# Attention by pairs of heads: scores in row halves of the array, feature-major values, bias tables by VectorE

## The chip, the cores and the metric

One core of one Trainium2 chip runs the whole program. The metric is device time in microseconds (us). All arithmetic is fp32, or fp32 split into a high and a low part (fp32r, "hi" and "lo", three matmuls for one product).

## The reference

Two layers of a trunk over 512 latent tokens (an 8 x 64 grid) of width 1024, with 256 context tokens. Layer 0 runs a state-space part (S5) beside neighbourhood attention with 8 heads of 64; layer 1 is a Fourier mixing. Each layer ends in a squared-ReLU MLP. The change concerns the attention alone:

```
scale = DH ** -0.5
s_lat = jnp.einsum('brqhd,brkhd->bhrqk', qg, k_blk).astype(f32) * scale + bias[None]
s_lat = jnp.where(mask, s_lat, NEG_INF)
s_ctx = jnp.einsum('brqhd,bkhd->bhrqk', qg, k_c).astype(f32) * scale
p = jax.nn.softmax(jnp.concatenate([s_lat, s_ctx], axis=-1), axis=-1).astype(v_l.dtype)
o = (jnp.einsum('bhrqk,brkhd->brqhd', p[..., :n_lat], v_blk)
     + jnp.einsum('bhrqk,bkhd->brqhd', p[..., n_lat:], v_c))
```

`bias` is a learned table by relative position, `mask` the window of 16 columns.

## The kernel before

**Stages.** After the norms, the projection by `w_in` (`qkv_gen`) runs on PE, interleaved with the S5 blocks (`s5_gen`), which are heavy on DVE. Then comes the attention (`na_gen`), interleaved with the gated unit of the S5 output (`glu_gen`) and with the loads and the row sum of one modulation vector (`side_gen`, `gemv_row`, tile `gacc`). Then the output projection (`wout_mm`, tile `po` with `whi`, `mh`), then the MLP. The order of the instructions on each engine is set by a scheduler from the order in which the generators emit them; every engine then works strictly in that order, waiting on semaphores.

**Attention.** The 512 queries are 4 column tiles (`ct`) of 128; each has 192 (`ct` 0 and 3) or 256 local keys and 256 context keys. One step of `scores` is one head: the tile `qP` holds each head's 64 features with zeros in the other 64 rows, so that q of one head times the 128 rows of two heads' keys gives one head's scores (L711 context, L712 local). DVE takes a minimum (L714), adds the bias table and takes the minimum again (L716); ACT takes the exponential (L717). `turn` transposes the 4 blocks of 128 keys on PE (L723, tile `ptp`) and ACT copies them (L724). `values` multiplies with the transposed scores as the stationary operand (L731, tile `po`). After 8 heads DVE divides by the sums (L735), and `to_mix` transposes to feature-major on PE (L741) and splits into hi and lo. PSUM has 3 banks for scores and outputs while S5 runs (`psum(mm=2, py=1, q=3)`), then 5.

**Bias tables.** Three tables are made once (L679 to L684): ACT copies the relative-position table with its sign turned, and POOL issues a DMA that adds the mask, broadcast over 8 heads, onto it from DRAM. The tables and the work tiles lie in the two large tiles `fh` and `fl`, which hold the projection's input (`lh`, `ll`) until its last matmul. The third large tile, `acc` (`RM`), holds the raw table; later the GLU's operand `gHL` takes its place.

**Weight slots.** `W.raw` has two slots of 1 MB in this stage. Four blocks of `w_mod` (each read by two DVE multiply-adds, L209) go through them, then the quarters of `w_out`, which ACT casts (L66) and DVE subtracts (L70).

Of the kernel before, what the change touches and what calls it, by code (L numbers as in the profile page):

```python
# [19 lines left out]
S = 512  # L20
# [73 lines left out]
def trunk(tc, I, out, dump=None):  # L94
# [15 lines left out]
    with es:  # L110
# [336 lines left out]
        qP = gp.tile([128, 4, 2, S], F32, name="qP")  # L447
# [24 lines left out]
        def qkv_gen():  # L472
            for grp in (4, 5, 6, 7, 2, 3):
                if grp == 2:
                    for b in range(2):
                        P.memset(qP[b * 64:b * 64 + 64, :, 1 - b], 0.0)
# [4 lines left out]
                if kind in "qk":  # L481
                    for m in range(2):
# [4 lines left out]
                        if kind == "q":  # L487
                            for b in range(2):
# [29 lines left out]
        def s5_params(b):  # L518
# [17 lines left out]
            qf = qP.rearrange("p m b n -> p (m b n)")  # L536
# [4 lines left out]
            if b == 2:  # L541
                CA = qf[:, 1024:2176].rearrange("p (c g e h) -> p c g e h", c=2, g=4, e=9)
            else:
                CA = s5b.tile([128, 2, 4, 9, 16], F32, tag="CA", name="CA", bufs=2)

# [127 lines left out]
        def na_gen():  # L673
            RM = big("acc", F32, "RM")
            SY.dma_start(RM[:, 0:2048], I["rb"])
            Rv = RM[:, 0:2048].rearrange("p (h a f) -> p h a f", a=4, h=8)
            N0, N1 = big("fh", F32, "N0"), big("fl", F32, "N1")
            bias = []
            for v, a0, na, bt in ((0, 1, 3, N0[:, 2048:3584]), (1, 0, 4, N0[:, 0:2048]), (2, 0, 3, N1[:, 0:1536])):  # L679
                bt = bt.rearrange("p (h n) -> p h n", h=8)  # L680
                A.activation(bt, Rv[:, :, a0:a0 + na].rearrange("p h a f -> p h (a f)"), AF.Copy, scale=-1.0)
                P.dma_start(bt, I["mask"][:, v, None, a0 * 64:(a0 + na) * 64].to_broadcast([128, 8, na * 64]),
                            accum_op=ADD)
                bias.append(bt)  # L684
            ots = [N0[:, 2048 + i * 512:2560 + i * 512] for i in range(4)]
            pes = [N1[:, 1536 + i * 512:2048 + i * 512] for i in range(3)]
            pTs = [N1[:, 3072 + i * 512:3584 + i * 512].rearrange("p (j n) -> p j n", j=4) for i in range(2)]
# [14 lines left out]
            def scores(i):  # L702
                ct, h = divmod(i, 8)
                bt, nl, k0, _ = cts[ct]
                w = nl + C
                if h == 0:
                    sums[ct] = sml.tile([128, 8], F32, tag="sm", name="sm")
                mt = h // 2
                sc = ps_q("sc")
                qs = qP[:, mt, h % 2, ct * 128:ct * 128 + 128]  # L710
                T.matmul(sc[:, nl:w], qs, kcT[:, mt], start=True, stop=True)  # L711
                T.matmul(sc[:, 0:nl], qs, kT[:, mt, k0:k0 + nl], start=True, stop=True)  # L712
                nc_ = sml.tile([128, 1], F32, tag="nc", name="nc")
                V.tensor_reduce(nc_, sc[:, nl:w], AX.X, MIN)  # L714
                nm = sml.tile([128, 1], F32, tag="nm", name="nm")
                V.tensor_tensor_reduce(sc[:, 0:nl], sc[:, 0:nl], bt[:, h], 1.0, nc_, ADD, MIN, nm)  # L716
                A.activation(pes[i % 3][:, 0:w], sc[:, 0:w], AF.Exp, bias=nm, scale=-1.0,  # L717
                             accum_out=sums[ct][:, h:h + 1])

            def turn(i):  # L720
                pt = ps_t("ptp").rearrange("p (j n) -> p j n", j=4)
                for j, (o, _, _) in enumerate(cts[i // 8][3]):
                    T.transpose(pt[:, j], pes[i % 3][:, o:o + 128], ident)  # L723
                A.copy(pTs[i % 2], pt)  # L724

            def values(i):
                ct, h = divmod(i, 8)
                if h == 0:
                    outs[ct] = ps_q("po").rearrange("p (h d) -> p h d", h=8)
                for j, (_, kn, vv) in enumerate(cts[ct][3]):  # L730
                    T.matmul(outs[ct][:, h], pTs[i % 2][0:kn, j], vv[:, h * 64:h * 64 + 64], start=(j == 0), stop=(j == 3))  # L731
                if h == 7:
                    rs = sml.tile([128, 8], F32, tag="rs", name="rs")
                    V.reciprocal(rs, sums[ct])
                    V.tensor_tensor(ots[ct].rearrange("p (h d) -> p h d", h=8), outs[ct],  # L735
                                    rs[:, :, None].to_broadcast([128, 8, 64]), MULT)

            def to_mix(ct):
                pt = ps_t("pto").rearrange("p (j n) -> p j n", j=4)
                for j in range(4):  # L740
                    T.transpose(pt[:, j], ots[ct][:, j * 128:j * 128 + 128], ident)  # L741
                split_to(mix["h"][:, 4:8, ct * 128:ct * 128 + 128], mix["l"][:, 4:8, ct * 128:ct * 128 + 128], pt)

            for i in range(38):
                if i < 32:
                    scores(i)
                if 2 <= i < 34:
                    turn(i - 2)
                if 3 <= i < 35:
                    values(i - 3)  # L750
# [670 lines left out]
```

## Time and profile before

| what | value |
|---|---|
| median of 3 runs | 1210.82 us (1207.87 to 1211.56) |
| the profiled execution's own time | 1216.72 us |
| its span | 1214.7 us |
| PE busy | 1154.9 us, 95% of the span |
| DVE, ACT busy | 756.6 us (62%), 502.0 us (41%) |
| mean granted TensorE clock | 0.982 |
| DMA | 171.60 MB, mean 141 GB/s |

The profiled execution lies 2.0 us above its span and 5.9 us above the median. A record of a timeline covers a run of like instructions; the distance from one start to the next is what an instruction costs in a full pipe, and the duration in the record is longer, since matmuls overlap. An fp32 matmul is two records (two passes), a transpose one.

### The profile page before, as it was taken

To read this page: it belongs to the slowest core of one execution; us is meant where nothing else is said; L and a number is where in the kernel's file an instruction comes from. 1 tells how busy PE (TensorE), PEld (TensorE's weight loads), DVE (VectorE), ACT (ScalarE), POOL (GpSimd) and SP (SyncE) were. 2 spreads that over 40 slices of the span, in tenths; PEclk is the share of its full clock that TensorE was granted. 3 is DMA by queue.
4 is the path that set the end of the run, shared out by engine and by line. 5 is a ranking of instruction groups with operands and counts; after the bars stand their busy time and mean duration, and the time that the engine had idled before them with its cause. 6 is when DMAs were issued, how large, how long until landed. Compare 5 with 4: busy or idle time off the path is not lost. (4 is left out here: it accounts for less than half of the span.)

```text
span 1214.7 us, 15755 instructions
## 1 busy us (share of the span) xinstructions
PE 1154.9 (95%) x6330; PEld 944.3 (78%) x6330; DVE 756.6 (62%) x1126; ACT 502.0 (41%) x825; POOL 89.8 (7%) x138
## 2 busy tenths in 40 slices
PE   5998999959999999999999999988999999999997
PEld 2687788747988888888888887867988888888886
DVE  7557999438447765775775546978674444344345
ACT  6664345448534753332232233357643223223322
POOL 1001332210001100000000000212000000000001
PEclk9998999979999999999999999998999999999999
DMA  6606444586048655465555421343362322232201
GB/s 257 235 27 187 118 127 108 152 177 201 1 169 294 214 208 174 158 223 173 185 197 173 151 93 70 99 196 105 105 242 104 104 81 94 104 104 74 100 1 69
DMA packets 45343, 171.60 MB, mean 141 GB/s; under 512 B 12619, under 2 KB 16976, under 8 KB 32854
## 3 DMA queue, kind: packets, MB, share of 16 engines
q1 hardware_dynamic: 38438, 154.78, 36.6%
q0 software_dynamic: 5824, 14.09, 5.7%
q10 hardware_dynamic: 1008, 1.72, 0.4%
q8 instruction: 49, 0.80, 0.3%
q14 instruction: 24, 0.20, 0.1%
HBM read 163.84 MB, written 6.75 MB: 140 GB/s over the span
## 5 line engine op out<-in xcount | busy, mean ns | idle before, releaser
L66 ACT CAST whi<-wraw 128x2048 fp32r<-128x2048 f32 (+2 forms) x103 | 147.8, 1459 | 294.0 <-PE pff L108 175.2
L70 DVE TENSOR_TENSOR wlo<-wraw,whi 128x2048 fp32r<-128x2048 f32 (+2 forms) x80 | 159.0, 1997 | 119.5 <-ACT whi L66 119.1
L106 PE MATMUL pff<-whi,ah 128*128 128x512 f32 (+1 forms) x482 | 189.2, 394 | 0.0
L108 PE MATMUL pff<-whi,al 128*128 128x512 f32 (+1 forms) x482 | 189.2, 393 | 0.0
L107 PE MATMUL pff<-wlo,ah 128*128 128x512 f32 (+1 forms) x482 | 188.9, 393 | 0.0
L993 DVE TENSOR_TENSOR facc<-facc,pff 128x512 f32<-128x512 f32 (+1 forms) x113 | 76.6, 680 | 93.7 <-PE pff L108 93.6
L209 DVE SCALAR_TENSOR_TENSOR gacc<-wraw,cs,gacc 128x1024 f32<-128x1024 f32 x76 | 97.4, 1282 | 29.6 <-DMA wraw<-w_mod 26.1
L107 PE MATMUL pf<-f1fl,whi 128*128 128x512 f32 (+1 forms) x288 | 106.4, 373 | 2.1 <-DVE f1fl L185 1.2
L106 PEld LDWEIGHTS pff<-whi,ah 128*128 128x128 f32 x482 | 90.5, 188 | 21.5 <-DVE facc L993 0.4
L108 PEld LDWEIGHTS pff<-whi,al 128*128 128x128 f32 x482 | 90.5, 188 | 21.3
L106 PE MATMUL pf<-f1fh,whi 128*128 128x512 f32 (+1 forms) x288 | 105.4, 374 | 1.7 <-ACT f1fh L185 1.3
L107 PEld LDWEIGHTS pff<-wlo,ah 128*128 128x128 f32 x482 | 90.5, 188 | 20.9
L107 PE MATMUL pf<-f0fl,whi 128*128 128x512 f32 (+1 forms) x288 | 105.5, 371 | 1.2 <-DVE f0fl L892 1.0
L108 PE MATMUL pf<-f1fh,wlo 128*128 128x512 f32 (+1 forms) x288 | 105.8, 371 | 0.0
L108 PE MATMUL pf<-f0fh,wlo 128*128 128x512 f32 (+1 forms) x288 | 105.0, 368 | 0.0
L106 PE MATMUL pf<-f0fh,whi 128*128 128x512 f32 (+1 forms) x288 | 103.4, 372 | 0.7 <-ACT rl L977 0.4
L977 ACT ACTIVATE rl<-pf 128x512 f32<-128x512 f32 (+1 forms) x72 | 38.9, 547 | 117.1 <-PE pf L108 110.1
L979 DVE TENSOR_TENSOR rl<-rl 128x512 f32<-128x512 f32 (+1 forms) x72 | 44.9, 628 | 57.5 <-ACT ah L978 52.1
L180 POOL TENSOR_TENSOR rstd<-ms,mhalf 128x1 f32<-128x1 f32 x33 | 29.8, 904 | 537.7 <-ACT ms L178 536.1
L107 PEld LDWEIGHTS pf<-f1fl,whi 128*128 128x128 f32 x288 | 54.7, 190 | 12.5 <-DVE f1fl L185 1.6
L106 PEld LDWEIGHTS pf<-f1fh,whi 128*128 128x128 f32 x288 | 54.1, 191 | 12.6 <-ACT f1fh L185 1.8
L108 PEld LDWEIGHTS pf<-f1fh,wlo 128*128 128x128 f32 x288 | 54.7, 190 | 10.1
(458 smaller groups left out, 2178.5 us busy)
## 6 DMA issues: line engine op xcount, KB each, us to landing
wraw<-w_ff SPq DMA_DIRECT2D x64, 1024.0 KB
wraw<-w_mod SPq DMA_DIRECT2D x40, 1024.0 KB
wm<-mod SPq DMA_DIRECT2D x8, 1024.0 KB
wraw<-w_in SPq DMA_DIRECT2D x8, 1024.0 KB
wlo<-w_in POOLq DMA_DIRECT2D x5, 1024.0 KB, 9.1
wraw<-w_out SPq DMA_DIRECT2D x4, 1024.0 KB
M<-kd POOLq DMA_DIRECT2D x32, 64.0 KB, 2.2
G<-norm_g SPq DMA_DIRECT2D x4, 512.0 KB
```

Source lines behind the costliest of these rows:

```text
L66: self.nc.scalar.copy(hi[:, k], t[:, k])
L70: self.nc.vector.tensor_tensor(lo[:, k], t[:, k], hi[:, k].bitcast(F32), SUB)
L106: T.matmul(ps, lh, rh, start=start, stop=False)
L107: T.matmul(ps, lh, rl, start=False, stop=False)
L108: T.matmul(ps, ll, rh, start=False, stop=stop)
L180: P.tensor_tensor(r, ms, mhalf, ALU.pow)
L209: V.scalar_tensor_tensor(acc, w[:, j], cw, acc, MULT, ADD)
L977: A.activation(rl, pf, AF.Relu)
L979: V.tensor_tensor(rl, rl, rl, MULT)
L993: V.tensor_tensor(dst, dst, pt, ADD)
```

## The change

- q is kept as `qT`, two heads above one another, without zeros. `scores` takes a pair of heads: head `e` uses rows `e*64` to `e*64+63` of the array, and each of the two has a PSUM bank.
- `values` makes the values the stationary operand (64 columns) and the transposed scores the moving one (128 columns), so that the output is feature-major, head `e` in column half `e` of the array. The division by the sums then needs them along the free axis: a transpose of the reciprocals, a copy, four matmuls with a selector `sel`, a copy, and one product on DVE. `to_mix` has no transposes left.
- The bias tables are made by DVE (`add_mask`) from the raw table and a mask without the head axis, which DMA loads into SBUF. The first lies in `RM` itself, so it doesn't wait for `lh`; the transposed scores `pTs` now lie in `RM` too, and the copied reciprocals `rt`.
- The S5 stage uses `qT` for `Q` of three blocks; `CA` has 3 buffers instead of 2 and a borrowed place.
- The generators' shares: 6 steps (of 20) of the attention are emitted beside S5, before 12 (of 38); afterwards 1 step of it for each one of the GLU, before 2.

```
-                            for b in range(2):
-                                hb = slice(b * 64, b * 64 + 64)
-                                A.activation(qP[hb, mt, b], pt[hb], AF.Copy, scale=-0.125)
+                            A.activation(qT[:, mt], pt, AF.Copy, scale=-0.125)
...
+            SY.dma_start(RM[:, 3584:4032], I["mask"][:, 0:448])
+            bias = {}
+            def add_mask(v, a0, na, bt, mk):
+                V.tensor_tensor(bt.rearrange("p (h a f) -> p h a f", h=8, a=na),
+                                mk.rearrange("p (a f) -> p a f", a=na)[:, None].to_broadcast([128, 8, na, 64]),
+                                Rv[:, :, a0:a0 + na], SUB)
+                bias[v] = bt.rearrange("p (h n) -> p h n", h=8)
+            add_mask(0, 1, 3, RM[:, 2048:3584], RM[:, 3584:3776])
             N0, N1 = big("fh", F32, "N0"), big("fl", F32, "N1")
...
+            SY.dma_start(sel, I["sel"])
+            SY.dma_start(N0[:, 3584:3776], I["mask"][:, 448:640])
+            add_mask(1, 0, 4, N0[:, 0:2048], RM[:, 3776:4032])
+            add_mask(2, 0, 3, N1[:, 0:1536], N0[:, 3584:3776])
...
+            pes = [N1[:, 1536 + i * 512:2048 + i * 512] for i in range(4)]
+            pTs = [RM[:, i * 512:512 + i * 512].rearrange("p (j n) -> p j n", j=4) for i in range(4)]
...
+                sc = [ps_q("sc") for _ in range(2)]
+                hb = [slice(e * 64, e * 64 + 64) for e in range(2)]
+                for e in range(2):
+                    T.matmul(sc[e][:, nl:w], qT[hb[e], mt, ct * 128:ct * 128 + 128], kcT[hb[e], mt], start=True, stop=True)
+                for e in range(2):
+                    T.matmul(sc[e][:, 0:nl], qT[hb[e], mt, ct * 128:ct * 128 + 128], kT[hb[e], mt, k0:k0 + nl],
+                             start=True, stop=True)
...
                 for j, (_, kn, vv) in enumerate(cts[ct][3]):
-                    T.matmul(outs[ct][:, h], pTs[i % 2][0:kn, j], vv[:, h * 64:h * 64 + 64], start=(j == 0), stop=(j == 3))
+                    for e in range(2):
+                        h = 2 * mt + e
+                        T.matmul(outs[ct][e * 64:e * 64 + 64, mt], vv[:, h * 64:h * 64 + 64], pTs[i % 2 * 2 + e][0:kn, j],
+                                 start=(j == 0), stop=(j == 3))
+                if mt == 3:
                     V.reciprocal(rs, sums[ct])
+                    pr = ps_t("pr")
+                    T.transpose(pr[0:8, 0:128], rs, ident)
+                    rt = RM[0:8, 3584:3712]
+                    A.copy(rt, pr[0:8, 0:128])
+                    pr = ps_t("pr").rearrange("p (m n) -> p m n", m=4)
+                    for m in range(4):
+                        T.matmul(pr[:, m], sel[:, m], rt, start=True, stop=True)
+                    A.copy(ots[ct], pr)
+                    V.tensor_tensor(ots[ct], ots[ct], outs[ct], MULT)
...
-        interleave((s5_gen(), 100), (chain(qkv_gen(), glu_weights(), itertools.islice(na, 12)), 3))
+        interleave((s5_gen(), 100), (chain(qkv_gen(), glu_weights(), itertools.islice(na, 6)), 3))
...
-        interleave((na, 2), (glu_gen(), 1), (side_gen(), 1))
+        interleave((na, 1), (glu_gen(), 1), (side_gen(), 1))
```

The scheduler orders the engines anew. Three places are shown, each first as it was and then as it is; the line numbers of the changed kernel are its own.

**First place: DVE, where the scores begin.** `sc,nm` rows are the bias additions, `nc` the minima, `gacc` the multiply-adds of the modulation vector, L673 the bias tables of the change.

As it was, on DVE:

```order
L714 TENSOR_REDUCE nc<-sc 128x1 x3
L716 ISA sc,nm<-sc,N_2644,nc 128x192
L716 ISA nm 128x1
L716 ISA sc,nm<-sc,N_2644,nc 128x192
L716 ISA nm 128x1
L716 ISA sc,nm<-sc,N_2644,nc 128x192
L716 ISA nm 128x1
L800 SCALAR_TENSOR_TENSOR e_2895<-e_2895,gh 128x512
L714 TENSOR_REDUCE nc<-sc 128x1
L716 ISA sc,nm<-sc,N_2644,nc 128x192
```

As it is now, on DVE:

```order
L70 TENSOR_TENSOR wlo_2634<-wraw_2631,whi_2633 128x2048
L673 TENSOR_TENSOR N_2641<-RM 128x2048
L719 TENSOR_REDUCE nc<-sc 128x1 x2
L209 SCALAR_TENSOR_TENSOR gacc<-wraw_3420,cs,gacc 128x1024
L719 TENSOR_REDUCE nc<-sc 128x1
L721 ISA sc,nm<-sc,RM,nc 128x192
L721 ISA nm 128x1
L721 ISA sc,nm<-sc,RM,nc 128x192
L721 ISA nm 128x1
L673 TENSOR_TENSOR N_2642<-N_2641,RM 128x1536
L209 SCALAR_TENSOR_TENSOR gacc<-wraw_3420,cs,gacc 128x1024
```

One table now stands ahead of the first minima; one more table and two multiply-adds stand between them and the third bias addition. (On PE, the last 10 `py` matmuls and the 8 `yt` transposes of S5, which stood among and behind the first three heads' scores, now stand ahead of all scores.)

**Second place: DVE, at the subtraction of a quarter of `w_out` (L70).** L800/L802 (now L813/L815) are the GLU's elementwise products, L753 the new product with the reciprocals.

As it was, on DVE:

```order
L800 SCALAR_TENSOR_TENSOR e_2946<-e_2946,gh 128x512
L716 ISA sc,nm<-sc,N_2644,nc 128x256
L716 ISA nm 128x1
L70 TENSOR_TENSOR wlo_3452<-wraw_3449,whi_3451 128x1024 x2
L790 SCALAR_TENSOR_TENSOR gHL<-gh,gHL 128x512
L714 TENSOR_REDUCE nc<-sc 128x1
L802 SCALAR_TENSOR_TENSOR gh<-e_2947,gh 128x512
L714 TENSOR_REDUCE nc<-sc 128x1
L716 ISA sc,nm<-sc,N_2644,nc 128x256
```

As it is now, on DVE:

```order
L719 TENSOR_REDUCE nc<-sc 128x1
L721 ISA sc,nm<-sc,N_2641,nc 128x256
L721 ISA nm 128x1
L70 TENSOR_TENSOR wlo_3463<-wraw_3460,whi_3462 128x1024 x2
L753 TENSOR_TENSOR N_2641<-N_2641,po 128x512
L815 SCALAR_TENSOR_TENSOR gh<-e_2877,gh 128x512
L185 TENSOR_TENSOR ml<-N_2641,mh 128x4x128
L813 SCALAR_TENSOR_TENSOR e_2921<-e_2921,gh 128x512
L719 TENSOR_REDUCE nc<-sc 128x1
L815 SCALAR_TENSOR_TENSOR gh<-e_2922,gh 128x512
L721 ISA sc,nm<-sc,N_2641,nc 128x256
L721 ISA nm 128x1
```

The subtraction stood after 13 heads' bias additions and now stands after 10; behind it come most of the GLU's products.

**Third place: PE, in the second half of the attention.** `pz` are the GLU's matmuls.

As it was, on PE:

```order
L108 MATMUL pz<-gHL,wlo_2639 128x512
L106 MATMUL pz<-gHL,whi_2638 128x512
L731 MATMUL po<-vl,N_2645 128x64 x2
L731 MATMUL po<-vc,N_2645 128x64 x2
L723 MATMUL ptp<-ident,N_2645 128x128 x4
L107 MATMUL pz<-gHL,whi_2638 128x512
L731 MATMUL po<-vl,N_2645 128x64 x2
L731 MATMUL po<-vc,N_2645 128x64 x2
L711 MATMUL sc<-kcT,qP 128x256
L712 MATMUL sc<-kT,qP 128x256
```

As it is now, on PE:

```order
L729 MATMUL ptp<-ident,N_2642 128x128 x4
L740 MATMUL po<-RM,vl 64x128
L714 MATMUL sc<-kT,qT 128x256
L712 MATMUL sc<-kcT,qT 128x256
L714 MATMUL sc<-kT,qT 128x256
L729 MATMUL ptp<-ident,N_2642 128x128 x4
L740 MATMUL po<-RM,vl 64x128 x3
L740 MATMUL po<-RM,vc 64x128 x4
L712 MATMUL sc<-kcT,qT 128x256
L729 MATMUL ptp<-ident,N_2642 128x128 x4
```

Scores (64 rows), transposes (whole array) and values (64 columns) now alternate, with some pairs' scores apart; from the fifth pair's values on there are 57 such alternations. And the 48 `pz` matmuls, which stood among the heads, all stand behind the attention's last matmul; PE as it is now, there:

```order
L740 MATMUL po<-RM,vl 64x128 x3
L740 MATMUL po<-RM,vc 64x128 x4
L751 MATMUL pr<-RM,N_2642 128x128 x4
L228 MATMUL grow<-gacc,ones 128x512
L106 MATMUL pz<-gHL,whi_2633 128x512
L107 MATMUL pz<-gHL,whi_2633 128x512
L108 MATMUL pz<-gHL,wlo_2634 128x512
L106 MATMUL pz<-gHL,whi_2633 128x512
L228 MATMUL grow<-gacc,ones 128x512
```

Their operand `gHL` takes the place of `RM`, which `pTs` and `rt` now hold to the end of the attention.

## Rows read from the trace of the kernel before

**Rows 1.** View by windows: us, busy time of PE, PEld, DVE, ACT, POOL, clock, DMA

```profile
200.00:230.00 30.00, 28.92 (x256) 24.28 (x253) 22.14 (x41) 14.03 (x29) 6.45 (x12) 1.00 0.46 127
...
239.00:262.00 23.00, 9.42 (x55) 7.61 (x53) 3.45 (x12) 12.52 (x19) 5.66 (x4) 0.65 1.01 182
...
302.00:322.00 20.00, 20.00 (x133) 18.11 (x132) 9.86 (x28) 11.68 (x27) 0.00 (x0) 1.00 0.00 1
```

**Rows 2.** Timeline (start us, us, engine line op) of DVE, then of PE, at the stall

```profile
257.44 0.42 DVE L716 CUSTOM_DVE_ANT_0 sc<-sc,N,nc 128x192 f32<-128x192 f32 x1 [13.79 <-DMA N<-mask]
...
258.73 1.12 PE L723 MATMUL ptp<-ident,N 128*128 128x128 f32 x4 [11.03 <-ACT N L717]
```

**Rows 3.** Timeline of PE, matmuls of heads in column tiles 2 and 3

```profile
310.08 0.59 PE L712 MATMUL sc<-kT,qP 128*128 128x256 f32 x2
310.52 0.55 PE L731 MATMUL po<-vl,N 128*128 128x64 f32 x4
310.91 0.61 PE L731 MATMUL po<-vc,N 128*128 128x64 f32 x4
311.35 0.61 PE L723 MATMUL ptp<-ident,N 128*128 128x128 f32 x4
311.80 0.60 PE L711 MATMUL sc<-kcT,qP 128*128 128x256 f32 x2
...
336.99 0.69 PE L731 MATMUL po<-vl,N 128*128 128x64 f32 x4
337.61 0.66 PE L731 MATMUL po<-vc,N 128*128 128x64 f32 x4
338.10 0.61 PE L723 MATMUL ptp<-ident,N 128*128 128x128 f32 x4
```

**Rows 4.** Timeline of PE, matmuls on parts of the array; first scores

```profile
199.11 0.33 PE L580 MATMUL kp<-CA,Q 64*32 64x128 f32 x1
199.12 0.34 PE L582 MATMUL kp<-CA,Q 64*32 64x144 f32 x1
...
239.31 0.59 PE L711 MATMUL sc<-kcT,qP 128*128 128x256 f32 x2
...
240.16 0.66 PE L643 MATMUL py<-CA,St 128*64 128x128 f32 x8
...
240.87 0.61 PE L643 MATMUL py<-CA,St 128*64 128x128 f32 x8
241.40 0.70 PE L711 MATMUL sc<-kcT,qP 128*128 128x256 f32 x2
```

**Rows 5.** Timeline of DVE, 274 to 294 us

```profile
274.82 1.28 DVE L209 SCALAR_TENSOR_TENSOR gacc<-wraw,cs,gacc 128x1024 f32<-128x1024 f32 x1
...
289.19 2.36 DVE L70 TENSOR_TENSOR wlo<-wraw,whi 128x1024 fp32r<-128x1024 f32 x2
...
293.00 0.41 DVE L714 TENSOR_REDUCE nc<-sc 128x1 f32<-128x256 f32 x1
293.33 0.48 DVE L716 CUSTOM_DVE_ANT_0 sc<-sc,N,nc 128x256 f32<-128x256 f32 x1
```

**Rows 6.** Timeline of SP's queue, then of ACT: loads of w_out and their casts

```profile
276.12 15.78 SPq L54 DMA_DIRECT2D wraw<-w_out  x4
...
281.11 1.99 ACT L66 CAST whi<-wraw 128x1024 fp32r<-128x1024 f32 x2
...
288.11 1.99 ACT L66 CAST whi<-wraw 128x1024 fp32r<-128x1024 f32 x2 [0.25 <-DMA wraw<-w_out]
```

**Rows 7.** Timeline of PE, then of ACT: end of one GLU column block

```profile
315.84 0.39 PE L107 MATMUL pz<-gHL,whi 128*128 128x512 f32 x1
316.07 0.39 PE L108 MATMUL pz<-gHL,wlo 128*128 128x512 f32 x1
...
316.56 0.60 ACT L812 ACTIVATE tz<-pz 128x512 f32<-128x512 f32 x1 [2.26 <-PE pz L108]
```

**Rows 8.** Timeline of PE in the output projection, its fourth matmul

```profile
352.03 0.39 PE L106 MATMUL po<-whi,mh 128*128 128x512 f32 x1
```

More of the change, by code (lines that the diff above doesn't have):

```diff
@@ L702, in scores @@
             def scores(i):
-                ct, h = divmod(i, 8)
+                ct, mt = divmod(i, 4)
                 bt, nl, k0, _ = cts[ct]
                 w = nl + C
-                if h == 0:
+                if mt == 0:
                     sums[ct] = sml.tile([128, 8], F32, tag="sm", name="sm")
[L708 to L718, printed above, removed]
@@ new lines, in scores @@
+                for e in range(2):
[3 more added lines that the diff above has]
+                    h = 2 * mt + e
+                    nc_ = sml.tile([128, 1], F32, tag="nc", name="nc")
+                    V.tensor_reduce(nc_, sc[e][:, nl:w], AX.X, MIN)
+                    nm = sml.tile([128, 1], F32, tag="nm", name="nm")
+                    V.tensor_tensor_reduce(sc[e][:, 0:nl], sc[e][:, 0:nl], bt[:, h], 1.0, nc_, ADD, MIN, nm)
+                    A.activation(pes[i % 2 * 2 + e][:, 0:w], sc[e][:, 0:w], AF.Exp, bias=nm, scale=-1.0,
+                                 accum_out=sums[ct][:, h:h + 1])
@@ L726, in values @@
+            def turn(i):
+                for e in range(2):
+                    pt = ps_t("ptp").rearrange("p (j n) -> p j n", j=4)
+                    for j, (o, _, _) in enumerate(cts[i // 4][3]):
+                        T.transpose(pt[:, j], pes[i % 2 * 2 + e][:, o:o + 128], ident)
+                    A.copy(pTs[i % 2 * 2 + e], pt)
             def values(i):
-                ct, h = divmod(i, 8)
-                if h == 0:
-                    outs[ct] = ps_q("po").rearrange("p (h d) -> p h d", h=8)
+                ct, mt = divmod(i, 4)
+                if mt == 0:
+                    outs[ct] = ps_q("po").rearrange("p (m n) -> p m n", m=4)
@@ L730, in values @@
                 for j, (_, kn, vv) in enumerate(cts[ct][3]):
-                    T.matmul(outs[ct][:, h], pTs[i % 2][0:kn, j], vv[:, h * 64:h * 64 + 64], start=(j == 0), stop=(j == 3))
-                if h == 7:
+                    for e in range(2):
+                        h = 2 * mt + e
+                        T.matmul(outs[ct][e * 64:e * 64 + 64, mt], vv[:, h * 64:h * 64 + 64], pTs[i % 2 * 2 + e][0:kn, j],
+                                 start=(j == 0), stop=(j == 3))
+                if mt == 3:
@@ L744, in na_gen @@
-            for i in range(38):
-                if i < 32:
-                    scores(i)
[L747 to L750, printed above, removed]
-                if i >= 13 and (i - 13) % 8 == 0:
-                    done.append((i - 13) // 8)
+                    pr = ps_t("pr")
+                    T.transpose(pr[0:8, 0:128], rs, ident)
+                    rt = RM[0:8, 3584:3712]
+                    A.copy(rt, pr[0:8, 0:128])
@@ new lines, in values @@
+                    pr = ps_t("pr").rearrange("p (m n) -> p m n", m=4)
[3 more added lines that the diff above has]
+                    V.tensor_tensor(ots[ct], ots[ct], outs[ct], MULT)
+            for i in range(20):
+                if i < 16:
+                    scores(i)
+                if 1 <= i < 17:
+                    turn(i - 1)
+                if 2 <= i < 18:
+                    values(i - 2)
+                if i >= 7 and (i - 7) % 4 == 0:
+                    done.append((i - 7) // 4)
@@ L753, in na_gen @@
                 while done and mix:
-                    to_mix(done.pop(0))
+                    ct = done.pop(0)
+                    tk = slice(ct * 128, ct * 128 + 128)
+                    split_to(mix["h"][:, 4:8, tk], mix["l"][:, 4:8, tk], ots[ct])
                 yield
@@ L1359, in prepare @@
         mk[:, v] = np.where((k >= c0) & (k < c0 + 16), 0.0, 1e30)
-    a["mask"] = mk
+    a["mask"] = f(np.concatenate([mk[:, 0, 64:], mk[:, 1], mk[:, 2, 0:192]], 1))
+    a["sel"] = f(np.repeat(np.eye(8, dtype=np.float32), 64, 1).reshape(8, 4, 128))
     ch = np.arange(512).reshape(2, 4, 2, 2, 16).transpose(0, 3, 1, 2, 4).reshape(-1)
```

35 lines of the change are left out of this document (5 added, 30 removed).

## The prediction

> **What bounds the kernel now.** I read the share of each engine first: PE is busy for 1154.9 of 1214.7 us, so the time can fall only where PE stands idle or where it gets less work. Next the view by windows, stage by stage. The part that the change touches begins at 239.3 us, where the projection's last matmul gives way to the first scores [rows 4], and ends at 352.03, where the fourth matmul of the output projection starts, in steady pitch again [rows 8]. Three stretches differ there [rows 1]: in the S5 stage, 200 to 230, PE is busy for 28.92 of 30 us and DVE for 22.14; from 239 to 262 PE is busy for 9.42 of 23 at a mean clock of 0.65, with DMA at its full share; from 302 to 322 PE is full at clock 1.00 and DVE half idle. The timeline then says what the hole is [rows 2]: the first bias addition started at 257.44 after 13.79 us of idle DVE, ended by a DMA that adds the mask to a table; PE waited 11.03 us for the exponential behind it. So there are two questions: what replaces the hole, and what PE has left once it runs full.
>
> **Part 0, ahead of the scores.** In the S5 stage the copies of q by halves and the memsets go from ACT and POOL, which end nothing there. The first table (1536 columns) lands on DVE inside this stage: by the 2.36 us of 2048 columns [rows 5] (2.3 in a full pipe) it takes 1.7 us, and DVE's idle time of 7.9 us in 30 covers it; if it were not covered, 1.7 us would be the price. The mask's loads are small and issued early, against a DMA load of 0.46 [rows 1]: nothing. The last `py` matmuls (240.16 to 241.40, twenty records, 1.2 us [rows 4]) and the eight `yt` transposes (eight at .11, the price of `ptp` [rows 3]) stood in the hole and cost nothing; now they stand ahead of all scores. Scores begin 2.1 us later, at 241.4.
>
> **Part 1, from the scores to PE being full.** The 13.8 us wait goes. What is late next is DVE, which the order loads with: table 1 (2.3), two minima (.33 each [rows 5], .7), a multiply-add `gacc` (1.3), one more minimum, two bias additions (.35 each at 192 columns, .7); the first exponential can start 5.3 us after the scores, not 18. Then table 2 (1.7) and the second `gacc` (1.3): 8.3 us. This `gacc` frees a weight slot. The third block of `w_mod` is on its way for 5.0 us (issue to cast of a 1 MB quarter, 276.12 to 281.11 [rows 6]; a later cast waited for its DMA, so this is not ACT's doing): 13.3. Its two `gacc`, with a minimum, 2.9: 16.2. The slot takes a quarter of `w_out`, 5.5 with its issue: 21.7; its cast 2.0 [rows 6]: 23.7. The next quarter 5.5: 29.2; half of its cast 1.0, then DVE's subtraction of the quarter, 2.3 [rows 5]: 32.5. In DVE's new order this subtraction stands after ten heads' bias additions, and behind it stand the product with the reciprocals, `ml`, six GLU products (eight pieces of 512 columns, .6 each by half a `gacc`: 4.8) and four heads (.75 each, 3.0), and about 2 us in which the products wait for ACT. The fourteenth bias addition ends at 42.3, so it begins 41.9 us after the scores, at 283.3. Before it began at 293.33 [rows 5]. **Lead: 10.0 us**, not 13.8: the loads, not the mask, set the pace. Here DVE waiting for a DMA in the subtraction holds up scores that stand behind it, and PE idles for it.
>
> **Part 2, PE's rest.** From the fourteenth bias addition on, before, 293.33 to 352.03 took 58.7 us of nearly full PE. After, 1.0 us passes until that head's exponential is done (.4, and .6 by the `tanh` of rows 7); then PE has these pieces. Transposes of 20 heads (the last two of the fourteen among them) at .45 [rows 3]: 9.0. Scores of 14 heads (4 are already in PSUM): .44 for the context keys, .44 or .33 for 256 or 192 local ones [rows 3], 11.4 one after another. Two matmuls on different row halves start 10 ns apart where they are neighbours (`kp`, 64 rows each) [rows 4], but the order has many heads' scores apart; I take 10.1. Values of 11 pairs, 16 records each; the nearest rows are the `py` matmuls, which also use 64 columns of the array and move 128: (.53 - .14) / 8 = .049 a record [rows 4], so .8 a pair, 8.6. Before, a head took .39 + .44 [rows 3], so the 22 heads took 18. The new transposes and selector matmuls, three times: one transpose and four fp32 matmuls of 128 columns in two passes each, nine records at .11, 2.9. **Changes of tiling:** beside a 64-row matmul the values of a head took .62 + .49 against .39 + .44 [rows 3], .28 for two changes, .14 each. The order has 57 from the fifth pair on and a few ahead: 60, 8.4 us. Stalls between a pair's scores and its exponentials: 2. Sum 41.0.
>
> Then the GLU. Its 48 matmuls no longer fill gaps: they all stand behind the attention. `gHL` needs DVE's product after the last value (1.5 us until the first), 48 at .233 (315.84 to 316.07) [rows 7] are 11.2, the row sums 1.7, and three gaps, because `pz` has one bank: the last matmul of a block started at 316.07, the `tanh` that frees the bank ended at 317.16 [rows 7], so nearly 1 us each, 2.9. That is 17.3. Clock lost in these gaps: 2 (the stretch of 239 to 262 lost a third of its clock, with far longer gaps [rows 1]). The output projection's first three matmuls are .7. Sum 1.0 + 41.0 + 17.3 + 2 + .7 = 62.0, against 58.7: **3.3 us given back**. What PE saves in the values is spent on changes of tiling and on an exposed GLU.
>
> **Sum.** 10.0 - 3.3 = 6.7 us less, from the profiled execution's own 1216.72: 1210.0. That execution lies 5.9 us above the median of 1210.82, and a median is what I forecast: **1204**.
>
> The output projection after it and the MLP are the same instructions; the loads for them hang on DVE's subtraction in both kernels, so I expect their lead kept.
>
> **A rule against the change.** The rows price one change of tiling at .14 us. In a sentence beside it: the Trainium skill, "TensorEngine Tiling (Array Packing)", section "Tiling Modes", says that a change of tiling mode makes TensorE drain; the trace agrees, .28 for two. The same page, "Theoretical Speedup", promises up to twice the rate for a contraction of 64 rows; by that the scores would take 5.7 instead of 10.1, and the time would be about 1200. The order shows why I don't take it: few pairs stand side by side.
>
> **The rivals.**
> - **Cheap changes.** In the S5 stage alternations are frequent and PE shows no holes; if most changes cost nothing (8.4), and neither stalls nor clock are lost (4): 12.4 less, 1192. Against it stand the .62 and .49 of rows 3.
> - **Nothing gained.** Each change costs .28, as the pair of rows 3 would if only one of its two ends paid: 8.4 more, 1212. Or the ramp is longer: each load of part 1 waits for a queue, four loads by 2 us. No change within measurement.
> - **Slower: the clock.** This is the one that ends on the other side. Where PE had holes, it had a granted clock of 0.65 [rows 1], between the levels of 1.2 and 2.4 GHz, and the new order has many short holes. At the lower level the 41 us of part 2 would take 82. The gain is 6.7, a measurable loss begins 3.6 beyond it: from 10.3 us, a quarter of those 41 at the lower level, it is slower; half of them give 1224. For it: holes in alternations, waits for ACT and DVE. Against it: 302 to 322, with the same alternation of scores, transposes and values, ran at 1.00 [rows 1].
> - **The halves don't run together.** If a pair's values cost .104 a record, as the .39 + .44 for eight do now [rows 3], 11 pairs cost 9.7 more, and the scores 1.3: 1215. Rows 4 speak against it, `kp` on halves and `py` at .049.
>
> **How the numbers follow.** 0.3% is 3.6 us, about what a measurement of this kernel can tell from no change. Forecast .45, its own range 1198 to 1209 (part 1 within 4 us either way, changes of tiling .07 to .2). Cheap changes .20. Nothing gained .16. The clock .12. Halves alone .07. Faster than 1207.2 are nearly all of the forecast's cases and the cheap changes, less a tail: .62. Same: .16 and a part of the tail: .19. Slower: the last two, .19. The range from 1189 to 1217 leaves out the worse half of the clock's case and a bit below.
>
> **What would show it.** Right: DVE's idle time before its first bias addition is a few us and not by a mask; the 14th bias addition at about 283; the subtraction of `w_out` waits for its cast about 30 us after the first scores; `pz` alone at the end with three gaps of 1 us; the output projection's first matmuls at 343 to 345. A pitch of values near .05 and gaps at changes of .14 would show the prices right. Wrong: a granted clock under 0.9 between 285 and 340, or values of a pair over 1.2 us, or a first exponential later than 10 us after the scores.

## The result, and the profile after

The changed kernel takes 1219.82 us (median of 6 runs, 1217.70 to 1225.76), the kernel before beside it 1211.52: a ratio of 1.0083, with an interval of 1.0056 to 1.0110. It is slower, by 7 to 13 us, where 1204 was forecast, outside the range of 1189 to 1217. The profiled execution (1225.76, span 1224.0) lies 5.9 us above its median, as that of before did, so the two profiles can be laid side by side; their spans differ by 9.3 us.

Windows of the changed kernel, with the columns of [rows 1]:

```profile
200.00:230.00 30.00, 30.00 (x283) 25.76 (x280) 29.00 (x53) 12.51 (x29) 6.27 (x10) 1.00 0.52 141
239.00:262.00 23.00, 18.29 (x109) 13.76 (x108) 16.00 (x27) 10.27 (x23) 0.00 (x0) 0.85 0.50 160
302.00:322.00 20.00, 19.91 (x164) 14.44 (x162) 8.97 (x30) 12.02 (x31) 0.00 (x0) 1.00 0.00 1
...
400.00:416.00 16.00, 7.46 (x35) 6.66 (x34) 7.30 (x13) 8.98 (x19) 3.96 (x4) 0.59 0.95 291
```

and the last of them in the kernel before:

```profile
400.00:416.00 16.00, 14.77 (x121) 14.14 (x119) 12.24 (x18) 10.80 (x26) 2.54 (x4) 1.00 0.69 255
```

The hole of 239 to 262 is gone: PE is busy for 18.29 of 23 us instead of 9.42. But there is a new one, behind everything that the prediction looked at: from 400 to 416 PE is busy for 7.46 us at a clock of 0.59, where the kernel before has 14.77 us at 1.00 in the same stretch. The places on the way, from the two timelines:

| us from the span's start | before | after |
|---|---|---|
| first matmul of the q, k, v projection | 92.83 | 94.94 |
| first scores | 239.31 | 244.44 |
| first bias addition | 257.44 | 248.96 |
| fourteenth bias addition | 293.33 | 289.60 |
| attention over, GLU's matmuls over | 350.31 (both) | 334.70, 350.96 |
| fourth matmul of the output projection | 352.03 | 351.67 |
| first Fourier matmul (`pf`) | 401.23 | 408.43 |
| end | 1214.7 | 1224.0 |

(The first line differs by chance: it lay between 89.8 and 95.2 in the executions of this study, whatever the kernel.) At the output projection the changed kernel is 0.4 us ahead, 2.5 with an equal start, where 6.7 was forecast. From there to the end it loses 9.7 us: 862.7 became 872.3. That is the result.

The rows that answer to [rows 2, 5, 8], of DVE and PE:

```profile
248.96 0.41 DVE L721 CUSTOM_DVE_ANT_0 sc<-sc,RM,nc 128x192 f32<-128x192 f32 x1
250.24 1.22 PE L712 MATMUL sc<-kcT,qT 64*128 64x256 f32 x2 [4.01 <-ACT N L722]
...
276.59 2.36 DVE L70 TENSOR_TENSOR wlo<-wraw,whi 128x1024 fp32r<-128x1024 f32 x2 [3.76 <-ACT whi L66]
289.60 0.48 DVE L721 CUSTOM_DVE_ANT_0 sc<-sc,N,nc 128x256 f32<-128x256 f32 x1
...
351.67 0.39 PE L106 MATMUL po<-whi,mh 128*128 128x512 f32 x1
```

The first bias addition waits for no mask and PE's wait for the first exponential is 4.01 us instead of 11.03 (here it is the next scores that wait, for the PSUM bank that the exponential frees); the subtraction of a quarter waits 3.76 us for its cast, with scores queued behind it.

Where the new hole comes from, step by step, on ACT, PE, DVE and SP's queue (start, duration, and in brackets the idle time before and what ended it):

```profile
334.87 1.67 ACT L802 ACTIVATE gHL<-gh 128x512 fp32r<-128x512 f32 x3 [2.21 <-PE pr L751]
350.74 0.39 PE L108 MATMUL pz<-gHL,wlo 128*128 128x512 f32 x1
350.94 2.00 ACT L66 CAST whi<-wraw 128x1024 fp32r<-128x1024 f32 x2 [1.50 <-PE pz L107]
352.02 2.36 DVE L70 TENSOR_TENSOR wlo<-wraw,whi 128x1024 fp32r<-128x1024 f32 x2 [1.86 <-ACT whi L66]
354.41 0.38 SPq L54 DMA_DIRECT2D wraw<-w_mod  x1
...
406.01 1.90 ACT L66 CAST whi<-wraw 128x2048 fp32r<-128x2048 f32 x1 [5.75 <-DMA wraw<-w_ff]
408.43 1.22 PE L106 MATMUL pf<-f0fh,whi 128*128 128x256 f32 x4 [7.15 <-ACT f0fh L903]
```

and the cast, the subtraction, the load and the first Fourier matmul in the kernel before:

```profile
331.88 1.99 ACT L66 CAST whi<-wraw 128x1024 fp32r<-128x1024 f32 x2 [1.75 <-PE pz L107]
332.96 2.36 DVE L70 TENSOR_TENSOR wlo<-wraw,whi 128x1024 fp32r<-128x1024 f32 x2 [2.29 <-ACT whi L66]
335.35 0.38 SPq L54 DMA_DIRECT2D wraw<-w_mod  x1
...
401.23 0.63 PE L106 MATMUL pf<-f0fh,whi 128*128 128x256 f32 x4
```

The GLU's operand `gHL` waits for the last selector matmul (`pr`, which reads `rt` in `RM`), so the GLU's matmuls run from 335.55 to 350.96, with only a row sum among them. A quarter of `w_out` is cast into the weight slot that the GLU's weights held, and its cast waits for the last `pz` (350.94, before 331.88). Only when DVE has subtracted it is its slot of `W.raw` free, and the first `w_mod` load goes out at 354.41 instead of 335.35. From 355 to 410 DMA is then busy for 0.90 of the time; ACT waits 5.75 us for a load of `w_ff`, and in its order that cast stands ahead of the Fourier operand: PE waits 7.15 us and then works at half its clock until about 416.

### The profile page after: what moved, and what is told of

Read it like the earlier page. It is cut to its first block, busy times and chain, and to the rows that moved or that the text cites. A ratio compares the mean times of both kernels' runs of the same rounds, so it can differ in the third digit from the quotient of the medians.

```text
span 1224.0 us, 15804 instructions
## 1 busy us (share of the span) xinstructions
PE 1164.3 (95%) x6350; PEld 933.5 (76%) x6350; DVE 762.5 (62%) x1129; ACT 498.4 (41%) x826; POOL 87.7 (7%) x133
## 4 chain that ended last, share of the span: by engine, by line
PE 83%; DVE 5%; DMA 5%; ACT 3%; issue 2%; SPq 0%; POOL 0%; ACTq 0%; DVEq 0%; POOLq 0%
PE pf L107 10%; PE pf L108 10%; PE pff L106 10%; PE pf L106 10%; PE pff L108 10%; PE pff L107 10%; PE po L740 2%; PE pq L106 2%; PE pq L107 2%; PE pq L108 2%; DMA wraw<-w_mod 1%; PE py L635 1%; PE ptp L729 1%; DVE gacc L209 1%; PE pv L604 1%
## 5 line engine op out<-in xcount | busy, mean ns | idle before, releaser
L70 DVE TENSOR_TENSOR wlo<-wraw,whi 128x2048 fp32r<-128x2048 f32 (+2 forms) x80 | 159.0, 1997 | 131.9 <-ACT whi L66 131.6
L107 PE MATMUL pf<-f1fl,whi 128*128 128x512 f32 (+1 forms) x288 | 106.7, 374 | 2.4 <-DVE f1fl L185 1.6
L108 PEld LDWEIGHTS pff<-whi,al 128*128 128x128 f32 x482 | 90.5, 188 | 21.2
L180 POOL TENSOR_TENSOR rstd<-ms,mhalf 128x1 f32<-128x1 f32 x33 | 34.4, 1044 | 557.6 <-ACT ms L178 556.0
L106 PEld LDWEIGHTS pf<-f0fh,whi 128*128 128x128 f32 x288 | 53.8, 193 | 17.7 <-ACT f0fh L903 7.4
```

What stands on the lines that cost most here:

```text
L70: self.nc.vector.tensor_tensor(lo[:, k], t[:, k], hi[:, k].bitcast(F32), SUB)
L106: T.matmul(ps, lh, rh, start=start, stop=False)
L107: T.matmul(ps, lh, rl, start=False, stop=False)
L108: T.matmul(ps, ll, rh, start=False, stop=stop)
L180: P.tensor_tensor(r, ms, mhalf, ALU.pow)
```

## The experiments

Ratios are to the kernel before, run on the same chip in the same job, with 95% intervals.

**e1: the GLU's operand free early.** `pTs` and `rt` of the pairs that come after the S5 stage get a tile of their own (8 KB of each partition, which `qP` had left).

```diff
+        late["pT"] = nab.tile([128, 4, 4, 128], F32, name="pTl", bufs=1)
+        late["rt"] = nab.tile([8, 128], F32, name="rtl", bufs=1)
...
-                    A.copy(pTs[i % 2 * 2 + e], pt)
+                    pT[i, e] = late["pT"][:, i % 2 * 2 + e] if late else pTs[i % 2 * 2 + e]
+                    A.copy(pT[i, e], pt)
```

> The changed kernel, but the transposed scores and the copied reciprocals of the pairs emitted after the S5 stage lie in a tile of their own, so that the GLU's operand gets its place after the first pairs. Theory 1 (the late GLU: the cast of the third w_out quarter waits for the GLU's last matmul, at 350.9, so a weight slot is freed at 354.4 instead of 335.3, the stream of w_mod and w_ff loads ends later, and PE stands idle for 7.2 us before the Fourier matmuls and then runs at half clock): the GLU's matmuls stand among the heads, the first w_mod load after w_out is issued before 340, no idle time over 2 us before the first pf; 1203 to 1210 us. Theory 2 (the pairs themselves cost, by changes of tiling and stalls, and the hole has another cause): the hole or as much stays, 1216 to 1222.

Measured: 1209.98 us, 0.9967 (0.9943 to 0.9991). `pz` begins at 285.14, the first `w_mod` load goes out at 323.73, no idle time ahead of the first `pf`:

```profile
323.73 0.38 SPq L54 DMA_DIRECT2D wraw<-w_mod  x1
...
391.31 0.64 PE L106 MATMUL pf<-f0fh,whi 128*128 128x256 f32 x4
```

One tile's place turns the change from 0.8% slower to 0.3% faster. Theory 1 holds, theory 2 falls as the cause of the loss; that the gain is half of the forecast one is left for e5 and e9.

**e3: the reverse, in the kernel before.** Only the two `pTs` move, from `N1` to `RM`.

```diff
-            pTs = [N1[:, 3072 + i * 512:3584 + i * 512].rearrange("p (j n) -> p j n", j=4) for i in range(2)]
+            pTs = [RM[:, 2048 + i * 512:2560 + i * 512].rearrange("p (j n) -> p j n", j=4) for i in range(2)]
```

> The kernel before, only that the two tiles of transposed scores lie in the tile whose place the GLU's operand takes, so that the GLU comes behind the attention as in the changed kernel. Theory 1: first w_mod load after w_out at 350 or later instead of 335, a hole of 5 to 15 us before the first pf, 8 to 20 us slower than before: 1219 to 1231. Theory 2: within 4 us of before (1208 to 1215).

Measured: 1224.5 us, 1.0101 (1.0070 to 1.0133). The first `w_mod` load goes out at 351.92, and around the first `pf` PE waits 1.27, 0.31, 4.95 and 0.84 us:

```profile
351.92 0.38 SPq L54 DMA_DIRECT2D wraw<-w_mod  x1
...
405.76 0.58 PE L107 MATMUL pf<-f0fl,whi 128*128 128x256 f32 x1 [4.95 <-DVE f0fl L892]
```

With not one matmul changed, the place of a work tile costs as much as the whole change did.

**e2, e7 and e8: is it the slot?** These keep the GLU as late as it is and load one quarter of `w_out` elsewhere, so that its late cast holds no slot: e2 the third quarter into a tile of its own, e7 the third into the place of a dead bias table, e8 the second there.

```diff
+            self.n["wraw"] += 1
+            t = raw.rearrange("p (a b) -> p a b", a=n0)
+            self.nc.sync.dma_start(t, src)
...
-                          parts=2 if i < 3 else 1)
+                          parts=2 if i < 3 else 1, raw=N0s[0][:, 0:2048] if i == 1 else None)
```

> The changed kernel with the GLU as late as it is, but the third quarter of w_out is loaded into a tile of its own instead of a weight slot, so that its late cast holds no slot. Theory 1: w_mod loads start some 10 to 20 us earlier than 354, the idle time of 7.2 us before the first pf falls below 3, and the time to 1207 to 1214. Theory 3 (the late GLU costs by standing exposed behind the attention, not by the slot): 1217 to 1222, the same as the changed kernel. Theory 2: the same, 1217 to 1222.

> The changed kernel with the GLU as late as it is; the third quarter of w_out is loaded into the first bias table of N0 (dead after its last bias addition, near 306), so that its late cast holds no weight slot, and the turn of the slots stays as it was (e2 changed the turn too, and its w_mod loads started no earlier). Theory 1: the first w_mod load and the loads of h start between 300 and 340 instead of 354, the idle time before the first pf falls from 7.2 to under 3, and the time to 1208 to 1214 beside a before of 1212. Rival (the late GLU costs by what VectorE has behind it, whatever the slots do): first pf as late as before, 1217 to 1224.

> e2 and e7 moved the wrong quarter of w_out: in the order of VectorE the quarter whose cast comes last is the second one, so their slot was still held until 350. Here the changed kernel loads the second quarter into the first table of N0 (dead near 306), the GLU stays as late as it is. Theory 1 (the late GLU holds a weight slot, and this holds back the loads): w_mod loads and the loads of h start before 330, two or three MB are in before the out-projection, the idle time before the first pf falls from 7.2 to under 3, first pf within 52 us of the out-projection's first matmul (57.5 in the changed kernel, 50.9 before); 1207 to 1214 beside a before of 1212. Rival (what stands behind the late products on VectorE sets it): first pf 56 us or more behind, 1217 to 1222.

Measured: e2 1223.84, 1.0087 (1.0069 to 1.0105); e7 1219.86, 1.0033 (1.0000 to 1.0067); e8 1213.28, 0.9974 (0.9950 to 0.9998). The first two were aimed at the wrong quarter: the third is cast early (at 308.82 in e7), the second is the one behind the GLU. In e2 one `w_mod` load left at 262.91, but the last quarter of `w_out` only at 348.70 and the next `w_mod` load at 351.58; in e7 the first `w_mod` load left at 350.73. They serve as controls: like e8 they have 1 MB of place more than the changed kernel, and it doesn't bring the time back (e7 lies between, with executions from 1211.33 to 1223.27, and its interval overlaps the changed kernel's). In e8 SP's queue and PE read:

```profile
258.65 0.37 SPq L54 DMA_DIRECT2D wraw<-w_mod  x1
317.09 1.75 SPq L953 DMA_DIRECT2D h<-xP  x4
349.72 0.38 SPq L54 DMA_DIRECT2D wraw<-w_mod  x1
395.16 0.73 PE L111 MATMUL pf<-f0fh,whi 128*128 128x256 f32 x4
396.92 0.38 PE L112 MATMUL pf<-f0fl,whi 128*128 128x256 f32 x1 [1.03 <-DVE f0fl L911]
399.35 0.39 PE L113 MATMUL pf<-f0fh,wlo 128*128 128x256 f32 x1 [2.05 <-DMA wlo<-w_ff]
```

One `w_mod` load and the four of `h` are out before the output projection, the first `pf` follows 49.5 us behind its first matmul (57.5 in the changed kernel), and what is left of the hole is 1.03 and 2.05 us. The GLU is as late and as exposed as before, and 13 us are back. So the held slot is what the late GLU costs. Its exposure (theory 3) moves the output projection, which starts 106.7 us after the first scores in e8 and 103.4 in e1, but the times (0.9974 and 0.9967) don't differ beyond their intervals.

**e4 and e6: the tables alone.** The kernel before with `add_mask` (edit as in the change, table 0 in `RM`), heads one by one; e6 repeats it.

> The kernel before, only with the three bias tables made by VectorE from a mask loaded into SBUF, the first in the raw table's tile. The 13.8 us wait before the first bias addition goes. Theory 1: with the GLU among the heads the lead of 5 to 10 us lasts to the end: 1201 to 1207. Rival (what is gained at the start is lost to weight slots, as loads set the pace afterwards): 1208 to 1213.

> The kernel of e4 again (heads one by one, tables by VectorE), with more rounds and on the same chip as e5, so that the two are compared. Theory that the pairs as they are ordered in e1 save nothing: e4's 0.993 of before comes again (0.990 to 0.996), below e1's 0.997. If the pairs save when they stand together: e5 is under it by 4 to 10 us; if not, e5 is within 3 us of it or above.

Measured: e4 1205.97, 0.9927 (0.9904 to 0.9950); e6 1206.95, 0.9947 (0.9926 to 0.9968). In e4's profile the first exponential ends a wait of 4.10 us instead of 11.03, the output projection starts 103.2 us after the first scores (111.0 before), and that lead lasts. The tables are the good half of the change. The rest of the change, pairs included, adds nothing to it: e1, which has all of it, is at 0.9967, 2 to 5 us above (the intervals overlap).

**e5: pairs that stand together.** A pair's two score tiles become one tile of two banks, so PE takes its four matmuls in a row.

```diff
-                sc = [ps_q("sc") for _ in range(2)]
+                if late:
+                    s2 = banks[2].tile([128, 1024], F32, tag="sc", name="sc", bufs=2)
+                    sc = [s2[:, 0:512], s2[:, 512:1024]]
+                else:
+                    sc = [ps_q("sc") for _ in range(2)]
...
-        psum(mm=1, q=5)
+        psum(mm=1, q=1, sc=2)
```

(`late` holds for the pairs after the S5 stage.)

> The kernel of e1, but after the S5 stage a pair's two score tiles are one tile of two PSUM banks, so that the four score matmuls of a pair stand next to each other on PE (before, most heads' scores stood alone, and PE spent as long on them as the kernel before: 28.2 against 28.2 us). If row halves run together only as neighbours (four matmuls in .53 us where a lone head takes .54 for two): PE's time for scores between the first scores and the output projection falls from 28 to 18 to 20 us, changes of tiling from 94 to about 60, and the kernel is 8 to 14 us faster than e1, 1196 to 1204 beside a before of 1212. Rival (DVE, ACT and the weight loads set the pace, PE's savings turn into idle time): PE's score time falls, its idle time rises by the same, within 3 us of e1.

Measured: 1207.61 us, 0.9938 (0.9913 to 0.9963); 2 to 4 us below e1 (the intervals overlap), no more than e4; 8 to 14 us below e1 were expected. PE's time from the first scores to the output projection by kind (distance from one start to the next, less idle time, summed over the timeline, us; the changes are those that the merged rows print, e11's kernel comes below):

| | scores | transposes | values | selector or `pto` | idle | changes of tile form |
|---|---|---|---|---|---|---|
| before | 28.2 | 15.4 | 32.1 | 2.1 | 17.1 | 18 |
| after | 28.6 | 21.4 | 25.2 | 6.3 | 11.1 | 86 |
| e4 | 28.8 | 16.0 | 32.8 | 1.8 | 8.6 | 18 |
| e1 | 28.2 | 21.2 | 26.7 | 6.3 | 7.2 | 94 |
| e5 | 26.5 | 24.2 | 28.8 | 6.4 | 9.9 | 80 |
| e11 | 21.8 | 27.7 with the added work | 21.9 | 5.2 | 9.6 | 88 |

In the changed kernel scores cost what they did. A part of that is the clock (with it up, in e12 below, they take 24.7 in the same count). Its timeline of PE, at full clock, shows the other part:

```profile
315.60 0.66 PE L729 MATMUL ptp<-ident,N 128*128 128x128 f32 x4
316.19 0.54 PE L740 MATMUL po<-RM,vl 128*64 128x128 f32 x5
...
317.21 0.70 PE L712 MATMUL sc<-kcT,qT 64*128 64x256 f32 x2
317.74 0.48 PE L714 MATMUL sc<-kT,qT 64*128 64x192 f32 x2
...
318.75 0.43 PE L740 MATMUL po<-RM,vl 128*64 128x128 f32 x2
319.11 0.66 PE L729 MATMUL ptp<-ident,N 128*128 128x128 f32 x4
319.69 0.54 PE L740 MATMUL po<-RM,vl 128*64 128x128 f32 x5
...
321.28 0.71 PE L712 MATMUL sc<-kcT,qT 64*128 64x256 f32 x4
321.81 0.50 PE L714 MATMUL sc<-kT,qT 64*128 64x192 f32 x4
322.24 0.80 PE L740 MATMUL po<-RM,vl 128*64 128x128 f32 x6
322.97 0.66 PE L740 MATMUL po<-RM,vc 128*64 128x128 f32 x8
323.56 1.15 PE L751 MATMUL pr<-RM,N 8*128 8x128 f32 x8
```

A lone head's two records take .53 (317.21 to 317.74), a pair's four take .53 as well (321.28 to 321.81): the halves do run side by side, but only as neighbours, and most pairs weren't. The transposes between them take .59 and .58 against .45 [rows 3]: one change of tiling each, .14. But e5 should have come out far lower, and its windows show what stood in the way: its clock.

**e9 and e10: the clock.** The stretch from 255 to 290, in which PE is busy for over 30 of the 35 us, in e4, in the changed kernel and in e5:

```profile
255.00:290.00 35.00, 31.25 (x200) 26.39 (x199) 27.37 (x62) 26.06 (x53) 0.94 (x1) 1.00 0.69 211
```

```profile
255.00:290.00 35.00, 30.37 (x178) 20.79 (x175) 21.66 (x45) 21.96 (x44) 0.94 (x1) 0.74 0.68 202
```

```profile
255.00:290.00 35.00, 30.70 (x138) 20.78 (x137) 20.50 (x44) 23.14 (x45) 0.95 (x1) 0.55 0.51 151
```

Heads one by one (e4) run at 1.00, the changed kernel at 0.74, e5 at 0.55. e9 takes e4 and, of the pairs, only the 64 rows in the score matmuls:

```diff
-                qs = qP[:, mt, h % 2, ct * 128:ct * 128 + 128]
-                T.matmul(sc[:, nl:w], qs, kcT[:, mt], start=True, stop=True)
-                T.matmul(sc[:, 0:nl], qs, kT[:, mt, k0:k0 + nl], start=True, stop=True)
+                hb = slice(h % 2 * 64, h % 2 * 64 + 64)
+                qs = qP[hb, mt, h % 2, ct * 128:ct * 128 + 128]
+                T.matmul(sc[:, nl:w], qs, kcT[hb, mt], start=True, stop=True)
+                T.matmul(sc[:, 0:nl], qs, kT[hb, mt, k0:k0 + nl], start=True, stop=True)
```

e10 takes e5 and adds matmuls of the whole array, overwritten by the transposes:

```diff
+                    for _ in range(3 if 0 <= i < 11 else 0):
+                        T.matmul(pt, onesr, onesr[:, None].to_broadcast([128, 4, 128]), start=True, stop=True)
```

> The kernel of e4 (heads one by one, tables by VectorE), and of the pairs only the row halves: the score matmuls take the 64 rows of their head instead of 128 rows with zeros, nothing else is moved. In the pair kernels the granted clock stays at .50 for 20 to 40 us from about 250 on although PE is busy there, in e4 it is back at 1.00 by 256. Theory A (the clock follows how much of the array the work uses; half-array scores are part of what keeps it down): the mean clock from 250 to 290 falls under .85 (1.00 in e4), and the time is 2 to 8 us above e4's. Theory B (the clock follows PE's idle times alone): the clock there as in e4, above .95; the time within 3 us of e4, plus changes of tiling (four a head, .14 each, 12 to 16 us of PE work at most, less what runs side by side).

> The kernel of e5 with work added that changes no result: before the transposes of each of the first 22 heads, three matmuls of 128 rows by 128 columns by 512 (ones by ones) go into the same PSUM tile and are overwritten. It costs 66 x .23 = 15 us of PE at full clock. Theory A (clock by use of the array): the clock from 255 to 290 rises from .50 to above .8, and the time is within 3 us of e5 or up to 8 below it in spite of the added work. Theory B (by idle times alone): the clock stays near .50 there, the added work costs 31 us of PE at the lower level, and the time rises by 8 to 20 us.

Measured: e9 1228.52, 1.0118 (1.0080 to 1.0156); e10 1215.23, 1.0002 (0.9972 to 1.0032). The same stretch, in e9 and in e10:

```profile
255.00:290.00 35.00, 35.00 (x114) 26.17 (x114) 16.58 (x33) 16.73 (x31) 0.94 (x1) 0.50 0.63 183
```

```profile
255.00:290.00 35.00, 30.00 (x202) 21.05 (x204) 21.28 (x46) 23.08 (x46) 0.94 (x1) 0.98 0.60 178
```

e9 is 21 to 23 us slower than e4 for leaving out 64 rows of zeros. In both the clock fell to 0.50 in the wait of 4.10 us before the first exponential. In e4, whose scores take all 128 rows, it was back at 1.00 from 254 on; in e9 it stayed at 0.50 until 301, through 56 us in which PE had no idle time at all. The mean clock of whole executions agrees: 0.960 to 0.965 in the four of e9, 0.981 to 0.990 in the four of e4. With whole-array work added (e10) it is 0.98 over the stretch, in spite of idle times of 0.3 to 1.3 us; but the added work is some 15 us of PE (an estimate: 66 matmuls of .23), and the time is about 8 us above e5's, where theory A had expected at most 3. Theory B, that idle time alone decides, falls in both. e9's time itself was outside what theory A gave it (2 to 8 us): I had not thought that it would last so long. Two things are not separated here. The 21 to 23 us hold the price of the new changes of tiling as well (an estimate: two a head at .14, 9 us for 32 heads). And whether it is the unused rows or those changes that kept the clock down stays open: before it rose, PE had run without either, in e9 from 296.60 to 300.10 (values and transposes on 128 rows; it rose near 301.5) and in the changed kernel from 280.45 to 283.86 (scores of neighbouring pairs, both halves in use; it rose near 283.5).

**e11 and e12: the clock for less.** The same added matmuls, but 16 in the wait before the first transposes and two a head in the next four pairs; on e5 (e11) and on the changed kernel (e12).

> The kernel of e5 with the added matmuls of e10 (ones by ones, overwritten by the transposes) only where PE is about to be idle or has just been: 16 between the second pair's scores and the first transposes (3.7 us, where PE waits 4 us for the first exponential anyhow), and two ahead of the transposes of each head of pairs 2 to 5 (16, 3.7 us). Theory A (once fallen, the clock does not come back while the work uses half the array): the clock from 245 to 290 stays above .9, the out-projection starts 100 to 104 us after the first scores (110 in e5), and the time is 3 to 10 us below e5: 0.985 to 0.991 of before. Theory C (ACT, DVE and the loads set the pace there, the clock costs nothing): clock up, time within 3 us of e5.

> The changed kernel as it is (late GLU, a slot held) with the added matmuls of e11. Theory A: the clock from 262 to 282 rises from .50 to above .9, the attention's last matmul comes 4 to 9 us sooner after the first scores (89.2 in the changed kernel); since the loads still hang on the GLU's end, all behind it moves by the same: 1.001 to 1.005 of before instead of 1.008. Theory C: clock up, 1.007 to 1.010.

Measured: e11 1204.10, 0.9923 (0.9896 to 0.9949); e12 1220.98, 1.0059 (1.0036 to 1.0083). The clock rose in both, to 0.91 and 0.95 from 255 to 290 (in e11 it fell once more, to 0.50 in 285 to 290, behind waits of 2.09 and 1.86 us). The score time in e11 fell to 21.8 us and the output projection starts 101.2 us after the first scores instead of 110. But the times move by less than expected, and within the intervals: e5's 0.9938 to 0.9923, the changed kernel's 1.0083 to 1.0059; in e12 the attention's last matmul comes 89.0 us after the first scores, no sooner than the changed kernel's 89.2. There the added work, and perhaps DVE and the loads, take what the clock gives; the runs don't part them. How much of the changed kernel's time the clock costs is therefore not settled: e12 is about 3 us lower with the added work in it, and the two intervals overlap.

## Why the prediction was wrong

**The step that failed** is the last sentence of the sum: that the loads behind the output projection "hang on DVE's subtraction in both kernels, so I expect their lead kept". The subtraction that they hang on hangs itself on the GLU, by the weight slot, and the GLU was forecast to move behind the attention. I had the late GLU in the sum, with its 17.3 us on PE (16.3 measured), and asked of it only what it costs PE, not what waits for it on ACT. The `pz` rows of the third place of the change name `whi_2633` and `wlo_2634`, the slot in question. e1, e3 and e8 show the price: 11 to 14 us.

**Part 0** was right in kind: 2.1 us forecast, 3.0 measured (149.5 against 146.5 us from the first projection matmul to the first scores). **Part 1** had its mechanism: the first bias addition came 4.5 us after the scores, not 18.1; the subtraction of a quarter began 32.2 us after them (30.2 forecast), waiting 3.76 us for the cast; the fourteenth bias addition came at 45.2 instead of 41.9, the lead was 3 us short. **Part 2**: 45.1 us from the fourteenth bias addition to the attention's end, 42.0 forecast. The clock is not the reason, nor are stalls:

```profile
289.60:334.70 45.10, 44.53 (x348) 30.83 (x348) 20.02 (x65) 27.89 (x69) 0.00 (x0) 1.00 0.01 1
```

PE had more work there than was counted. 64 score records were left, 16 heads and not 14, and most pairs stood apart. In the last column tile, where one block of keys has 64 rows, the second piece of a pair's values took 1.32 (322.24 to 323.56) and not 1.02: two more changes of tiling, as in the 64-row blocks of [rows 3]. Elsewhere the prices held, so that "Cheap changes" and "Nothing gained" fall: a change of tiling .14; a pair's values .36 + 1.02 with four changes, so .82 or .051 a record, .049 forecast. With the GLU 1.0 shorter than forecast, and without the 2 set aside for its clock, these terms (0.9, 3.3 and 3.1) are what lies between the 6.7 us and the 2.5 found at the output projection.

**The rivals.** "The clock" came true elsewhere than I put it. I put it into part 2 and named a clock under 0.9 between 285 and 340 as its sign; there it was 1.00. It stood at 0.50 from about 250 to 256 and from 267 to 283, in part 1, whose sum I had worked out at full clock, and in which the pairs' work was slow to bring it back. Those 23 us of half clock cost less than their price: part 1 ended 3.3 us late as a whole. The subtraction in it waited for its cast, and the cast for its load:

```profile
275.51 1.99 ACT L66 CAST whi<-wraw 128x1024 fp32r<-128x1024 f32 x2 [0.40 <-DMA wraw<-w_out]
```

Behind the subtraction DVE waited 2.23 us more (at 281.18) for a copy of what PE's selector matmuls had made at half clock; there the clock can have its share.

"The halves don't run together" was half right: they do, and stood apart. That a later wait would take the gain had no rival, and should have: I had named the waits of DVE for ACT and not followed ACT's for PE.

The Trainium skill, "TensorEngine Tiling (Array Packing)", section "Tiling Modes", says that a change of tiling mode drains the engine; this trace agrees, with .14 us for each. Its section "Theoretical Speedup" gives up to twice the rate at 64 rows; in this trace that holds for neighbours alone, whose four records take the .53 us of a lone head's two.

## What to carry to other kernels

When a step moves later, ask of every buffer that it reads when it is given back, and follow the next holder through its cast, its subtraction and its load: the price may stand 50 us further on, in a stage that the change doesn't touch. Before two half-array products are put in place of two padded ones, see in the trace that they will stand next to each other, and look at the granted clock: zeros that fill the array can be worth more than the rows they waste. The version to keep from this study is e4 (tables by VectorE, heads one by one), 0.5 to 0.7% faster than before; e11, which is as fast, needs padding work to be so.

## What was not expected of the hardware

TensorE stayed at 0.50 of its clock (1.2 of 2.4 GHz) for 56 us of unbroken work (e9, 245 to 301) in which scores on 64 rows alternated with whole-array transposes and with values, where the same sequence with the scores on 128 rows was back at 1.00 within 10 us (e4). A transpose record of four takes 1.11 us there and 0.60 in e4 at full clock, so the column of the clock can be believed. A PE that the profile shows as busy throughout says nothing of the clock that it runs at; the column of the granted clock has to be read beside it.
